# Low halves of plainly multiplied weight units: an adding transfer onto a negated copy instead of a subtraction on VectorE

## The chip, the cores and the metric

The kernel runs on one core of a Trainium2 chip. The metric is the device time of one execution in microseconds (us); lower is better. Engines are named as in the profile: PE (matmul) and PEld (its weight loads), DVE (VectorE), ACT (ScalarE), POOL (GpSimd), SP (SyncE, which issues most of the transfers here).

## The reference

One inference step of a decoder of two layers, for a prompt of 512 positions and a sample group of 8 x 8 positions, together 576 columns, with a model width of 1024. What matters here is where the large matrix products are:

```python
def sqrelu_mlp(x, w_up, w_down):
    return jnp.square(jax.nn.relu(x @ w_up)) @ w_down
...
    for l in range(DEPTH):
        i = l // 2
        if l % 2 == 0:
            y, s1, wk1, r1 = ab_mixer(x, ...)      # RWKV-7 heads and retention heads
        else:
            y, c1 = conv_mixer(x, ...)             # W_out(B * conv3(C * (W_in x)))
        x = layer_norm(ALPHA * x + y, ln1_g[l], ln1_b[l])
        x = layer_norm(ALPHA * x + sqrelu_mlp(x, w_up[l], w_down[l]), ln2_g[l], ln2_b[l])
```

The hidden width of the MLP is 4096. Inputs, weights and results are float32.

## The kernel before

**Precision.** PE multiplies operands of the type fp32r, a float32 that is rounded when it is written. To keep more of float32 every operand is held as a pair: `hi` is the value rounded to fp32r (a copy on ACT), `lo` is the value less `hi` (a subtraction on DVE). Both are made in `parts` (L72 to L79). A product of two pairs is three matmuls, in `mm3` (L150 to L154): hi by hi (L152), hi by the other's lo (L153), and the weight's lo by hi (L154). So a weight unit's `lo` is first read by the third matmul of its first step.

**Units.** The weights stand in HBM as units of 128 x 1024 numbers (512 KB), numbered in the order of use; a unit holds 8 blocks (k = 0 to 7) of 128 x 128 and makes 128 rows of a result. The columns are worked in two halves of 288 (g = 0, 1). A plain unit is 2 x 8 x 3 = 48 matmuls.

**Two phases.** Units 0 to 37 belong to the mixers of the first layer, a phase of its own that loads in half units; the change does not touch it. The second phase begins with unit 38 (`start_at(38)`, L1503): first MLP (38 to 101), convolution layer (102 to 133), second MLP (134 to 197). `mlp` (L1605) goes in four quarters, each with 8 units of the up-projection and 8 of the down-projection, and `res_evac` adds each result to the residual; the last unit of the last quarter is followed by a layer norm (`ln_add`, `ln_finish`).

**Plain and paired units.** Two units next to each other can be multiplied by a scheme with 7 products instead of 8 (`gemm7`, `steps7`), which needs sums of weight blocks. Such pairs are prepared in `prepare` (L117): POOL and DVE form sums at L123, then `parts` splits the results. All other units are multiplied as they are, in `gemm` (L156). Plain are the first four units of each MLP (38 to 41 and 134 to 137), all down-projections (46 to 53, 62 to 69, 78 to 85, 94 to 101, and the same in the second MLP), units 102 to 107 and 126 to 133 of the convolution layer. The up-projections of the quarters, and 108 to 125, are pairs.

**How a plain unit is prepared.** `gemm` calls `ensure` for units a little ahead; `ensure_` (L87) takes the next unit, gets a pair of buffers from `wtile` (or, for units 102 to 104 and 134 to 137, from `spots`, which are buffers of x that are free at that time), calls `load_to` (L48) so that SP loads up to three units ahead (L59) into three `raw` buffers, and calls `parts` on the raw copy. `parts` works in two chunks of four blocks (`chunk` is 4, from CH at L1285 and L1506): ACT copies 128 x 512 (L77), DVE subtracts 128 x 512 (L78), twice. In this phase there are five pairs of weight buffers `wh`, `wl` (WA + WB at L1291), which plain units use in turn with the pairs, and a pair of units takes three of them.

**The order of the work.** The tile framework orders each engine's instructions at build time with a simulated time line, by the order in which the code emits them and by when their operands are ready; on the chip each engine then works through its list in order, and semaphores hold it where an operand is late. So an instruction that waits holds up all that stand behind it on its engine. Preparation is emitted ahead of use and so tends to run as soon as a buffer comes free. `gate` (L83) keeps the preparations after a norm from running ahead of it.

**Where POOL works in this phase.** POOL makes the sums at L123 for the pairs, two of the seven combinations of each pair (L205), the subtractions of the mean at the norm (L255), its running sums (L273), products at L310, and sums of x at L1564. It issues few transfers: most are issued by SP.

Of the kernel before, what the change touches and what calls it, by code (L numbers as in the profile page):

```python
# [10 lines left out]
F32 = mybir.dt.float32  # L11
F32R = mybir.dt.float32r
AF = mybir.ActivationFunctionType
ALU = mybir.AluOpType
PSUM = bass.MemoryType.PSUM

P = 128
NT = 576
GN = 288
KT = 8  # L20
# [4 lines left out]
class Trunk:  # L25
# [61 lines left out]
    def ensure_(self, u, half=False):  # L87
        nc = self.nc
        u = min(u, self.nu - 1)
        while self.done <= u:  # L90
            if self.done in self.pairs:
                if self.half is None:
                    self.half = self.prepare(self.done)
                    next(self.half)
                if half: break
                for _ in self.half: pass
                self.half = None
                self.done += 2
                continue
            sp = []  # L100
            if self.halves:
                p = self.p_wsp[0]
                for h in range(2):
                    hi = p.tile([P, KT // 2, P], F32R, tag="wh", name="wh")
                    lo = p.tile([P, KT // 2, P], F32R, tag="wl", name="wl")
                    self.load_to(2 * self.done + h + 1)
                    self.parts(hi, lo, self.raw.pop((self.done, h)).rearrange("p (k m) -> p k m", m=P))
                    sp += [(hi[:, k], lo[:, k]) for k in range(KT // 2)]
            else:
                hi, lo = self.spots.get(self.done) or self.wtile()  # L110
                self.load_to(2 * self.done + 7)
                self.parts(hi, lo, self.raw.pop((self.done, 0)).rearrange("p (k m) -> p k m", m=P))
                sp = [(hi[:, k], lo[:, k]) for k in range(KT)]
            self.split[self.done] = sp
            self.done += 1
# [1595 lines left out]
```

## Time and profile before

| | |
|---|---|
| median of the runs shown | 1574.73 us (1573.41 to 1576.05, two runs) |
| the profiled execution | 1570.47 us |
| its span, first to last instruction | 1568.7 us |
| mean granted PE clock | 0.968 |
| second phase | from 484 us to the end |
| HBM read | 124.39 MB |

The profile records one execution. Three things help in reading it. An engine's share of busy time is an average over stages with different limits, so the windows by stage matter more. PE's matmuls overlap: a group's mean of some 297 ns is the time of one from start to end, while they start some 0.13 us apart at full clock. And what ended the idle time before an instruction is named behind it: `<-DMA raw<-in_w` means that a load into a raw buffer came last.

The tiles that the text names are `raw` (a loaded unit), `wh` and `wl` (hi and lo of a weight unit), `ht` and `lt` (hi and lo of a unit in one of the spots; the same names also stand for the sums of x), `hh`/`hl`, `he`/`le`, `ho`/`lo` (pairs of x or of hidden values), `acc` (a result in PSUM), `ln`, `u`, `x` (the norm).

### The profile page before, as it was taken

Reading aid. Unit: us, or ns where it says so; the run is one execution under the profiler, and the core shown is the slowest. Engines: PE = TensorE matmul, PEld = TensorE weight load, DVE = VectorE, ACT = ScalarE, POOL = GpSimd, SP = SyncE. Lnnn points to the kernel's source line nnn. Section 1 sums busy time; section 2 is a strip of 40 time slices with the busy share of each in tenths; the row PEclk is TensorE's granted clock in tenths of the full one; section 3 lists DMA queues with packets and bytes.
Section 4 is the critical chain, followed back from the end, with each engine's and each line's share of the span. In section 5 each row is a group of like instructions: output and inputs, shape, how many; then the busy total and the mean of one; then the engine's idle time right before and its main releaser. Section 6 shows DMA issues by size and latency. Waiting matters only on the chain.

```text
span 1568.7 us, 29898 instructions
## 1 busy us (share of the span) xinstructions
PE 1476.0 (94%) x11760; PEld 1421.9 (91%) x11760; DVE 1077.6 (69%) x2038; ACT 639.8 (41%) x1345; POOL 564.0 (36%) x643
## 2 busy tenths in 40 slices
PE   6999999998997889999999998989998999999995
PEld 6999898987886689999999997889988999999995
DVE  4656766675756795664846779899799575574755
ACT  4444334332233553342624545434365244251533
POOL 2032213336443551211302377555564121121355
PEclk9999999999898889999999999999999999999998
DMA  5333234435223013231322411223402314132221
GB/s 171 96 96 91 86 101 130 139 92 168 82 64 120 0 43 121 81 122 57 106 81 68 135 42 56 74 74 115 129 1 81 97 66 135 54 121 68 83 66 61
DMA packets 71197, 140.04 MB, mean 89 GB/s; under 512 B 21744, under 2 KB 31200, under 8 KB 71056
## 3 DMA queue, kind: packets, MB, share of 16 engines
q1 hardware_dynamic: 68224, 129.69, 26.6%
q0 software_dynamic: 1536, 5.57, 1.1%
q10 hardware_dynamic: 1296, 2.86, 0.6%
q8 instruction: 92, 1.51, 0.4%
q14 instruction: 49, 0.40, 0.1%
HBM read 124.39 MB, written 13.70 MB: 88 GB/s over the span
## 4 chain that ended last, share of the span: by engine, by line
PE 77%; DVE 11%; DMA 4%; POOL 4%; issue 3%; ACT 1%; SPq 1%; DVEq 0%; ACTq 0%; POOLq 0%
PE acc L152 21%; PE acc L153 21%; PE acc L154 21%; DVE wl L78 2%; PE mx L803 2%; DMA raw<-in_w 1%; DVE u L309 1%; POOL x L255 1%; DVE hl L78 1%; PE mx L700 1%; PE wa L152 1%; PE mx L542 1%; PE pq L283 1%; PE ps L283 1%; PE wa L154 1%
## 5 line engine op out<-in xcount | busy, mean ns | idle before, releaser
L77 ACT CAST wh<-raw 128x512 fp32r<-128x512 f32 x440 | 252.7, 618 | 411.2 <-PE acc L153 269.7
L78 DVE TENSOR_TENSOR wl<-raw,wh 128x512 fp32r<-128x512 f32 x440 | 330.2, 782 | 42.2 <-ACT wh L77 34.9
L153 PE MATMUL acc<-hl,wh 128*128 128x288 f32 x1180 | 349.0, 297 | 7.1 <-DVE hl L78 7.1
L154 PE MATMUL acc<-hh,wl 128*128 128x288 f32 x1180 | 348.6, 297 | 0.0
L152 PE MATMUL acc<-hh,wh 128*128 128x288 f32 x1180 | 344.4, 297 | 2.3 <-DVE ta L205 1.8
L153 PEld LDWEIGHTS acc<-hl,wh 128*128 128x128 f32 x1180 | 222.9, 189 | 8.0 <-DVE hl L78 7.5
L152 PEld LDWEIGHTS acc<-hh,wh 128*128 128x128 f32 x1180 | 221.2, 189 | 3.2 <-DVE ta L205 2.0
L154 PEld LDWEIGHTS acc<-hh,wl 128*128 128x128 f32 x1180 | 223.0, 189 | 0.3
L152 PE MATMUL acc<-xh,wh 128*128 128x288 f32 x480 | 148.3, 310 | 13.4 <-ACT xh L1395 12.4
L123 POOL TENSOR_TENSOR s<-raw 128x512 f32<-128x512 f32 x37 | 56.0, 1515 | 272.4 <-DMA raw<-in_w 206.1
L153 PE MATMUL acc<-xl,wh 128*128 128x288 f32 x480 | 146.2, 305 | 0.0
L154 PE MATMUL acc<-xh,wl 128*128 128x288 f32 x480 | 146.0, 304 | 0.0
L152 PE MATMUL acc<-ht,wh 128*128 128x288 f32 x444 | 130.9, 296 | 1.7 <-ACT wh L77 1.3
L153 PE MATMUL acc<-lt,wh 128*128 128x288 f32 x444 | 130.7, 295 | 0.0
L154 PE MATMUL acc<-ht,wl 128*128 128x288 f32 x444 | 130.5, 295 | 0.0
L123 POOL TENSOR_TENSOR raw<-raw 128x512 f32<-128x512 f32 x37 | 54.6, 1475 | 157.0 <-DVE raw L123 106.6
L152 PEld LDWEIGHTS acc<-xh,wh 128*128 128x128 f32 x480 | 91.5, 191 | 16.7 <-ACT xh L1395 12.8
L153 PE MATMUL acc<-lo,wh 128*128 128x288 f32 x352 | 105.2, 299 | 0.0
L152 PE MATMUL acc<-ho,wh 128*128 128x288 f32 x352 | 104.9, 300 | 0.1
L154 PE MATMUL acc<-ho,wl 128*128 128x288 f32 x352 | 104.9, 299 | 0.0
L153 PEld LDWEIGHTS acc<-xl,wh 128*128 128x128 f32 x480 | 91.5, 191 | 2.6 <-DVE xl L1396 0.7
L154 PEld LDWEIGHTS acc<-xh,wl 128*128 128x128 f32 x480 | 91.6, 191 | 1.5 <-issue 0.2
(461 smaller groups left out, 3498.0 us busy)
## 6 DMA issues: line engine op xcount, KB each, us to landing
raw<-in_w SPq DMA_DIRECT2D x160, 512.0 KB, 3.9
raw<-in_w SPq DMA_DIRECT2D x60, 256.0 KB, 2.9
A<-stg SPq DMA_DIRECT2D x9, 288.0 KB, 2.4
x<-in_x POOLq DMA_DIRECT2D x8, 288.0 KB, 7.4
out_y<-x SPq DMA_DIRECT2D x16, 144.0 KB, 1.8
wr<-in_w SPq DMA_DIRECT2D x16, 128.0 KB, 2.3
wr<-in_w SPq DMA_DIRECT2D x32, 64.0 KB, 2.0
kr<-A SPq DMA_DIRECT2D x6, 288.0 KB, 2.7
```

The costliest lines, as they stand in the source:

```text
L77: a = self.nc.scalar.copy(hi[:, s], src[:, s])
L78: b = self.nc.vector.tensor_tensor(out=lo[:, s], in0=src[:, s], in1=hi[:, s].bitcast(F32), op=ALU.subtract)
L123: tt = lambda e, o, x, y, op: e.tensor_tensor(out=o, in0=x, in1=y, op=op)
L152: nc.tensor.matmul(acc, lhsT=hi, rhs=xh, start=first, stop=False)
L153: nc.tensor.matmul(acc, lhsT=hi, rhs=xl, start=False, stop=False)
L154: nc.tensor.matmul(acc, lhsT=lo, rhs=xh, start=False, stop=last)
L255: e.tensor_tensor(out=t, in0=t, in1=c, op=ALU.subtract)
L283: self.nc.tensor.matmul(st[k], lhsT=self.ones1024, rhs=t, start=start, stop=stop)
L309: nc.vector.tensor_tensor(out=u, in0=r, in1=mn, op=ALU.subtract)
L542: self.nc.tensor.matmul(ps, lhsT=lhsT, rhs=rhs[:, o:o + n], start=True, stop=True)
L700: nc.tensor.matmul(both[h][:, i], lhsT=b3[q, c, h:h + 2].rearrange('p s t -> p (s t)'), rhs=la[q, c], start=True, stop=True)
L803: nc.tensor.matmul(ps[:, i], lhsT=bd(self.mb if n < 3 else self.Y0, j + i), rhs=v[:, j + i], start=True, stop=True)
```

## The change

For plain units of the second phase `lo` is made in another way. ACT copies the raw unit to `hi` as before, then writes the negative of `hi` into `lo` (a second ACT operation for each chunk). Then one transfer, issued by POOL, reads the same unit from HBM once more and adds it onto `lo` in place (`accum_op=ALU.add`), so that `lo` ends as the weight less `hi`. DVE has no part in it. The raw buffer is now released by ACT's copy and no longer by DVE's subtraction. The load into `raw` stays. Pairs, the splits of x and of hidden values, and the first phase go on with `parts`.

```diff
             else:
                 hi, lo = self.spots.get(self.done) or self.wtile()
                 self.load_to(2 * self.done + 7)
-                self.parts(hi, lo, self.raw.pop((self.done, 0)).rearrange("p (k m) -> p k m", m=P))
+                src = self.raw.pop((self.done, 0)).rearrange("p (k m) -> p k m", m=P)
+                for i in range(0, KT, 4):
+                    a = nc.scalar.copy(hi[:, i:i + 4], src[:, i:i + 4])
+                    nc.scalar.activation(lo[:, i:i + 4], hi[:, i:i + 4].bitcast(F32), AF.Copy, scale=-1.0)
+                b = nc.gpsimd.dma_start(lo.rearrange('p k m -> p (k m)'), self.w_all[self.done].bitcast(F32R), accum_op=ALU.add)
+                self.last = [a.ins, b.ins]
                 sp = [(hi[:, k], lo[:, k]) for k in range(KT)]
             self.split[self.done] = sp
             self.done += 1
```

## The prediction

> **What bounds the kernel now.** First the busy times of the whole span, then the same by stages, because an average hides where an engine waits. A row by stage gives the window, its length, then the busy time of PE, PEld, DVE, ACT and POOL, the granted clock, the DMA share and GB/s.
>
> ```profile
> PE 1476.0 (94%) x11760; PEld 1421.9 (91%) x11760; DVE 1077.6 (69%) x2038; ACT 639.8 (41%) x1345; POOL 564.0 (36%) x643
> ```
> ```profile
> 484.00:500.00 16.00, 11.41 (x59) 8.85 (x58) 11.98 (x24) 6.80 (x15) 3.37 (x8) 0.79 0.75 235
> ...
> 604.00:892.00 288.00, 288.00 (x2175) 287.79 (x2174) 177.73 (x303) 114.03 (x208) 57.46 (x50) 1.00 0.29 90
> ...
> 940.00:964.00 24.00, 16.70 (x100) 15.77 (x99) 23.93 (x31) 12.33 (x27) 19.33 (x18) 0.86 0.20 67
> ...
> 1204.00:1516.00 312.00, 312.00 (x2356) 311.79 (x2355) 197.94 (x336) 129.90 (x236) 65.14 (x58) 1.00 0.29 94
> ...
> sum 1085.00, PE 1024.85 PEld 1007.41 DVE 772.61 ACT 465.80 POOL 404.74; mean PE 68.32 PEld 67.16 DVE 51.51 ACT 31.05 POOL 26.98
> ```
>
> The change touches only the second phase, from 484 us on. In two long stages (288 and 312 us) PE never stops at full clock, while DVE works 62% and 63% of the time. Relief for DVE is worth nothing there. In all the phase PE is idle 1085 - 1025 = 60 us, around the layer norms and in the convolution; that is the ceiling of any gain, and 940 to 964 is a place where DVE is full (23.93 of 24) and PE is not.
>
> The weights are the second thing to read: who waits for them, and how long before PE needs them they are made.
>
> ```profile
> SPq L59 <- DVE wl L78: 889.6, 140, 75.0
> ```
> ```profile
> ACT wh L77 <- PE acc L153: 269.7, 108, 5.7
> ```
>
> The loads wait for DVE to release a raw slot; the casts wait for PE to release a pair of weight buffers. So a weight unit's preparation starts when PE frees a buffer, and the time from then to its first use is fixed by the five buffers, not by DVE.
>
> **What is removed.** In the issues below, 160 units are loaded in this phase, and the pair sums on POOL (L123) number 37, so 74 units go in pairs and 86 plainly. Each plain unit has two subtractions at L78.
>
> ```profile
> raw<-in_w SPq DMA_DIRECT2D x160, 512.0 KB, 3.9
> raw<-in_w SPq DMA_DIRECT2D x60, 256.0 KB, 2.9
> ```
> ```profile
> L77 ACT CAST wh<-raw 128x512 fp32r<-128x512 f32 x440 | 252.7, 618 | 411.2 <-PE acc L153 269.7
> L78 DVE TENSOR_TENSOR wl<-raw,wh 128x512 fp32r<-128x512 f32 x440 | 330.2, 782 | 42.2 <-ACT wh L77 34.9
> L123 POOL TENSOR_TENSOR s<-raw 128x512 f32<-128x512 f32 x37 | 56.0, 1515 | 272.4 <-DMA raw<-in_w 206.1
> ```
>
> 172 subtractions x 0.782 us = 134.5 us leave DVE, most of it in the stages where PE is full: worth nothing there. The two places where plain subtractions lie on the chain that sets the end are these (rows of the chain and of DVE):
>
> ```profile
> 949.49 3.12 ACT wh L77 x6
> ...
> 954.22 0.35 ACT ho L77
> 954.59 3.74 DVE wl L78 x3
> ...
> 961.18 1.53 DVE lo L78
> ```
> ```profile
> 1088.61 2.43 DVE wl L78 x2
> ...
> 1095.01 0.72 DVE wl L78
> ```
>
> At 949 units 105 to 107 are prepared ahead of the last splits of x, for which PE waits. Without the subtractions DVE is free for the splits, but ACT has six negations more (six x 0.57 = 3.4 us) ahead of the casts that these splits need; the last of those ends at 954.6, so now near 958.0, and the split that started at 961.18 starts there: **-3.2 us**. Bounds: 0 (POOL, with three issues between its sums, is late instead) and -7.4 (all six subtractions). At 1088 to 1095.7 the chain loses up to 2.43 + 0.72 = 3.2 us, but unit 126's own landing is due there; see below.
>
> **What is added.** On ACT, 172 negations 128x512. No such row exists; a cast of that size is 618 ns, two in a row take 1.14 us in the rows below, so 0.57 each, 98 us in all. ACT stands at 41% of the span, and in the long stages at 114 of 288 us: hidden by its idle time. On POOL, 86 issues at about 0.54 us (first row), 46 us in all; in the long stages POOL is busy 57 of 288 us: hidden too. On the DMA engines, 86 x 512 KB again; their share there is 0.29, so even at double price (source and destination read) there is room: hidden.
>
> ```profile
> L1427 POOL DMA_DIRECT2D x<-in_x x8 | 4.3, 541 | 5.1 <-PE acc L154 5.1
> ```
> ```profile
> s<-in_wkv POOLq DMA_DIRECT2D x4, 256.0 KB, 4.0
> ...
> lw<-in_lw POOLq DMA_DIRECT2D x1, 768.0 KB, 10.5
> ```
>
> **The disputed price: when does lo land?** No adding transfer is in the trace. From SP 256 KB land in 2.9 us and 512 KB in 3.9 us; from POOL 256 KB land in 4.0 us, so 1.1 us later than from SP. A plain 512 KB from POOL would then take 5.0 us. The adding one also reads its destination: 512 KB more through the same engines, at SP's step of 1.0 us per 256 KB, is 2.0 us. Bounds: 5.0 us (the second read hides) and 10.5 us (the slowest POOL row). I take 6.5 us, three quarters of the second read, because raw loads share the engines.
>
> The Trainium skill, page "DMA: Bandwidth & Descriptors", section "Anatomy of one DMA — SWDGE (gpsimd) path", fits a transfer issued by GpSimd as 2.0 us plus bytes over 436,000 per us, an estimate of 3.2 us for this size. The trace does not bear that out: 256 KB already take 4.0 us here. By that price nothing below would be late, and the sum would be near -4 us (-3.2, another -3.2 at 1088, +2.0 at the start).
>
> From the start of a unit's casts to lo ready I count four ACT operations of 0.57 us, POOL's issue of 0.54, and 6.5 us: 2.9 + 6.5 = **9.4 us**. Before it was cast, then subtraction, some 2.5 us. Now the lead, at each passage from pairs to plain units (start of the first unit's casts; PE's first use; lo is read two matmuls later, 0.27 us):
>
> ```profile
> 676.53 1.14 ACT L77 CAST wh<-raw 128x512 fp32r<-128x512 f32 x2 [0.44 <-PE acc L153]
> ...
> 585.18 1.12 ACT L77 CAST wh<-raw 128x512 fp32r<-128x512 f32 x2
> ...
> 1203.45 3.23 ACT L77 CAST wh<-raw 128x512 fp32r<-128x512 f32 x6
> ...
> 1087.64 1.14 ACT L77 CAST wh<-raw 128x512 fp32r<-128x512 f32 x2 [1.47 <-DMA raw<-in_w]
> ...
> 903.30 1.14 ACT L77 CAST wh<-raw 128x512 fp32r<-128x512 f32 x2
> ```
> ```profile
> 687.53 0.30 PE L152 MATMUL acc<-hh,wh 128*128 128x288 f32 x1
> ...
> 592.25 0.30 PE L152 MATMUL acc<-hh,wh 128*128 128x288 f32 x1
> ...
> 1212.23 0.30 PE L152 MATMUL acc<-hh,wh 128*128 128x288 f32 x1
> ...
> 1096.15 0.40 PE L152 MATMUL acc<-hh,wh 128*128 128x288 f32 x1 [1.81 <-DVE ta L205]
> ```
> ```profile
> 911.11 0.46 DVE L257 TENSOR_TENSOR x<-x,acc 128x288 f32<-128x288 f32 x1 [2.39 <-PE acc L154]
> ```
>
> Unit 62 (and its five likes, in the other quarters of the two MLPs) has 11.0 + 0.27 = 11.3 us: hidden, by 1.9 us. Unit 46 has 592.52 - 585.18 = 7.3: late by **+2.1**. Unit 142, the third of the casts that start at 1203.45 (so at 1205.6), has 6.9: late by **+2.5**. Unit 126 has 8.8: **+0.6**, and the chain's 3.2 us on DVE are lost with it. Unit 101, the last before the first MLP's closing norm, is cast at 903.30; PE gets to it when the product before it is done and taken by DVE, at 911.11, so it has 8.1 us: +1.3, and 0.5 for the operation that POOL may be in: **+1.8**.
>
> PE also pays for the stall itself. After a long wait the chain shows 0.24 us per matmul instead of 0.13 for some 20 matmuls:
>
> ```profile
> 560.32 2.42 DVE hl L78 x2
> ...
> 563.40 0.24 PE acc L154
> ...
> 568.20 0.24 PE acc L153
> ...
> 568.62 0.13 PE acc L152
> ```
>
> From 563.40 to 568.62 some 21 matmuls lose 0.11 us each, 2.4 us. I charge this once, at unit 142, the longest of the stalls: **+2.4**. Bounds: 0 and twice that.
>
> **The start of the phase**, 484 to 500, has the DMA engines at 0.75 already, and units 38 to 41 bring 2 MB more, though PE needs none of it until the norm is done. POOL is the risk: it works in order, and what waits behind an issue is the norm:
>
> ```profile
> 499.32 1.52 POOL L123 TENSOR_TENSOR s<-raw 128x512 f32<-128x512 f32 x1 [5.84 <-DMA raw<-in_w]
> 500.81 5.34 POOL L255 TENSOR_TENSOR x<-x,ln 128x288 f32<-128x288 f32 x7
> ```
>
> Here the pair sum already stood 5.84 us at the head of POOL's queue and held up the norm's subtractions. Bounds: -1.5 (raw slots come free after the cast, so that the sum comes sooner) and +5 (an issue waits for the fourth unit's negation, which waits for its load). I take **+2.0**.
>
> **The sum:** -3.2 + 2.1 + 2.5 + 0.6 + 1.8 + 2.4 + 2.0 = **+8.2 us**. The profiled execution took 1570.5 us (span 1568.7); it becomes 1578.7. The median of the runs shown is 4.2 us above the profiled one, so I predict **1582.9 us**, 0.5% more. A difference under 2% (31 us) is about what a measurement of this kernel can't tell from none.
>
> **Rivals.** *Late landings everywhere (slower).* If lo takes 11.0 us from issue to landing instead of 6.5, unit 62's kind is late by 2.9 + 11.0 - 11.3 = 2.6 us, and each of six such passages costs 2.6 + 2.4 = 5.0, together 30 us; the four short ones get 4.5 us worse each, 18 us, and two more slow starts add 4.8. With the sum of +8.2 that is +61: 1636 us. The six begin to pay from 8.4 us on, and 2% are passed near 9.5. For it: 10.5 us at 768 KB, and the loads that run at the same passages. Against it: 4.0 us at 256 KB. *In time everywhere (a gain).* If lo lands within 4 us of its issue, every lateness vanishes, and what is left is -3.2 at 949, up to -3.2 at 1088 and nothing at the start: -6, so 1569 us. For it: the DMA engines are idle for 0.7 of the long stages. Against it: the same 4.0 us for half the bytes. The fit of the Trainium skill's page named above would give this case. *POOL held up at the norms.* If each of the four norms finds an issue that waits for ACT at the head of POOL's queue, as the pair sum at 499.32 did, and loses those 5.84 us each time, it adds 23.4 us less the 2.0 counted: 1604 us. Against it: the issue waits for ACT alone, which is idle half of the time at a norm (12.33 of 24 us busy from 940), while the pair sum waited for a load.
>
> **Chances.** The forecast 0.55 (1570 to 1598); in time everywhere 0.18; late landings 0.18; POOL held up 0.09. No case gains 31 us, and half of the 60 us of idle time would be needed: faster 0.02. Late landings end above 1606 nearly always, POOL held up in a third of cases: slower 0.20. Same 0.78. The range runs from 1564 (the gain with its larger bound) to 1618, which leaves out the worse half of the late landings.
>
> **What would show it.** Right: L78's weight rows fall by 172, PE stays full from 604 to 892, DMA landings from POOL near 6.5 us, PE waits for a DMA into wl at 592 and 1212 only, each of 2 to 4 us. Wrong: PE waiting for wl at 687 and its likes; landings of 10 us; POOL's queue standing at the head of a norm; or issues on POOL far above 0.54 us.

## The result, and the profile after

The changed kernel takes 1614.4 us (median of two runs, 1613.64 to 1615.16) against 1574.73 before: 2.6% more, ratio 1.0261, 95% interval 1.0233 to 1.029. That is 39.7 us, against a forecast of 8.2. The profiled execution has a span of 1613.4 us (before 1568.7), 44.7 more. The edit adds five lines above the rest, so in the changed kernel the three matmuls of a product are L157 to L159, the norm's subtractions L260 and the sums of x L1569; the new cast, negation and transfer are L114, L115 and L116.

First the engines over the whole span and the rows of the lines that the change touches.

```profile
PE 1490.2 (92%) x11760; PEld 1434.1 (89%) x11760; DVE 953.4 (59%) x1866; ACT 726.7 (45%) x1517; POOL 617.9 (38%) x729
...
L78 DVE TENSOR_TENSOR wl<-raw,wh 128x512 fp32r<-128x512 f32 x282 | 211.2, 781 | 39.9 <-ACT wh L77 33.5
...
L116 POOL DMA_DIRECT2D wl<-in_w x79 | 71.1, 912 | 184.8 <-ACT wl L115 160.7
```

DVE is relieved as planned: 124 us less, 158 subtractions fewer in this row, and 14 more in the units of the spots. It bought nothing. POOL's issue takes 0.912 us where 0.54 was assumed. Then the transfers: size and median time from issue to landing, and the time that the software queue's packets took as a share of 16 engines.

```profile
raw<-in_w SPq DMA_DIRECT2D x160, 512.0 KB, 4.6
...
wl<-in_w POOLq DMA_DIRECT2D x79, 512.0 KB, 8.4
```
```profile
q0 software_dynamic: 13920, 50.67, 16.3%
```

Low parts land after 8.4 us, not 6.5, and SP's own loads became slower, 4.6 us instead of 3.9. Now by stages (window, length, busy PE, PEld, DVE, ACT, POOL, granted clock, DMA share, GB/s) and PE's waits for these transfers (us in total, times, longest).

```profile
606.00:620.00 14.00, 12.62 (x84) 12.62 (x85) 2.14 (x4) 3.32 (x6) 1.72 (x2) 0.88 1.01 239
622.00:904.00 282.00, 282.00 (x2133) 282.00 (x2133) 147.53 (x250) 135.01 (x250) 75.39 (x72) 1.00 0.52 135
...
1250.00:1264.00 14.00, 11.13 (x72) 10.90 (x73) 1.88 (x3) 7.17 (x14) 3.22 (x4) 0.88 1.05 283
1264.00:1558.00 294.00, 294.00 (x2220) 293.79 (x2219) 149.15 (x258) 142.93 (x265) 80.94 (x79) 1.00 0.52 133
```
```profile
PE acc L159 <- DMA wl<-in_w: 18.2, 6, 4.2
```

The two long stages are as full as before, at full clock. The loss sits in short stretches: behind the first passage of each MLP the DMA engines have no room left (share 1.01 and 1.05), and PE stalls, and its mean granted clock in these two windows is 0.88. Six waits, 18.2 us together, stand where there were none. The timeline of PE names all six: at 607.38 (unit 46), 936.07 (unit 101), 990.77 (105), 1123.49 (126), 1163.80 (133) and 1252.82 (142).

Around the closing norm of the first MLP the chain that sets the end (start, us, what) ran through POOL's norm operations before as well:

```profile
890.23 9.58 POOL x L255 x10
...
900.64 4.00 POOL x L255 x4
```

Now transfers stand behind them on it:

```profile
907.54 2.68 POOL x L260 x4
...
911.12 1.61 POOL x L260 x3
...
914.22 4.75 POOL x L260 x7
...
919.53 0.80 POOL wl L116
...
924.85 11.08 DMA wl<-in_w
...
974.85 6.83 POOL ts L1569 x8
...
985.27 5.46 DMA wl<-in_w
```

Fourteen norm operations come first on POOL. Unit 100 is issued behind them at 919.53, and three units for the spots go out before unit 101 at 924.85. It lands 11.08 us later, in a burst of five. Sixty us later the same happens behind the sums of x at L1569: unit 105 is issued behind them and PE waits for it.

### The profile page after: what moved, and what is told of

The parts are those of the page before. It is cut to its first block, busy times and chain, and to the rows that moved or that the text cites. A ratio compares the mean times of both kernels' runs of the same rounds, so it can differ in the third digit from the quotient of the medians.

```text
span 1613.4 us, 30164 instructions
## 1 busy us (share of the span) xinstructions
PE 1490.2 (92%) x11760; PEld 1434.1 (89%) x11760; DVE 953.4 (59%) x1866; ACT 726.7 (45%) x1517; POOL 617.9 (38%) x729
## 3 DMA queue, kind: packets, MB, share of 16 engines
q0 software_dynamic: 13920, 50.67, 16.3%
q10 hardware_dynamic: 1296, 2.86, 0.6%
## 4 chain that ended last, share of the span: by engine, by line
PE 69%; DVE 10%; DMA 7%; POOL 6%; issue 5%; ACT 2%; SPq 1%; DVEq 0%; ACTq 0%; POOLq 0%
PE acc L159 19%; PE acc L157 19%; PE acc L158 19%; DMA wl<-in_w 3%; PE mx L808 2%; DVE wl L78 2%; DMA raw<-in_w 2%; DVE u L314 1%; PE wa L157 1%; POOL ts L1569 1%; POOL ln L278 1%; PE mx L705 1%; PE wa L159 1%; POOL s L128 1%; DVE u L315 1%
## 5 line engine op out<-in xcount | busy, mean ns | idle before, releaser
L159 PE MATMUL acc<-hh,wl 128*128 128x288 f32 x1180 | 351.2, 300 | 15.5 <-DMA wl<-in_w 15.4
L157 PE MATMUL acc<-hh,wh 128*128 128x288 f32 x1180 | 344.3, 298 | 1.2 <-ACT hh L77 0.6
L159 PEld LDWEIGHTS acc<-hh,wl 128*128 128x128 f32 x1180 | 225.2, 191 | 17.3 <-DMA wl<-in_w 10.5
L78 DVE TENSOR_TENSOR wl<-raw,wh 128x512 fp32r<-128x512 f32 x282 | 211.2, 781 | 39.9 <-ACT wh L77 33.5
L157 PEld LDWEIGHTS acc<-hh,wh 128*128 128x128 f32 x1180 | 223.0, 191 | 2.2 <-ACT hh L77 0.9
L157 PE MATMUL acc<-xh,wh 128*128 128x288 f32 x480 | 148.2, 310 | 13.7 <-ACT xh L1400 11.6
L159 PE MATMUL acc<-xh,wl 128*128 128x288 f32 x480 | 146.1, 304 | 0.0
L116 POOL DMA_DIRECT2D wl<-in_w x79 | 71.1, 912 | 184.8 <-ACT wl L115 160.7
L157 PE MATMUL acc<-ht,wh 128*128 128x288 f32 x444 | 130.9, 296 | 2.7 <-ACT wh L77 1.7
L159 PE MATMUL acc<-ht,wl 128*128 128x288 f32 x444 | 130.5, 294 | 0.0
L114 ACT CAST wh<-raw 128x512 fp32r<-128x512 f32 x158 | 89.9, 617 | 84.0 <-PE acc L158 79.9
L157 PEld LDWEIGHTS acc<-xh,wh 128*128 128x128 f32 x480 | 91.4, 191 | 17.1 <-ACT xh L1400 12.0
L157 PE MATMUL acc<-ho,wh 128*128 128x288 f32 x352 | 105.4, 301 | 0.1
L159 PE MATMUL acc<-ho,wl 128*128 128x288 f32 x352 | 104.8, 298 | 0.0
```

The lines of the kernel that those rows point to most:

```text
L78: b = self.nc.vector.tensor_tensor(out=lo[:, s], in0=src[:, s], in1=hi[:, s].bitcast(F32), op=ALU.subtract)
L114: a = nc.scalar.copy(hi[:, i:i + 4], src[:, i:i + 4])
L116: b = nc.gpsimd.dma_start(lo.rearrange('p k m -> p (k m)'), self.w_all[self.done].bitcast(F32R), accum_op=ALU.add)
L157: nc.tensor.matmul(acc, lhsT=hi, rhs=xh, start=first, stop=False)
L159: nc.tensor.matmul(acc, lhsT=lo, rhs=xh, start=False, stop=last)
```

## The experiments

My theory after the result: the loss is lateness at the places with a short lead, made by a landing that is dearer than assumed and by POOL's order. Rivals: a price for every unit (traffic, ACT, POOL), the negations on ACT, or the adding itself. All edits below are to the changed kernel unless said otherwise. Each time is the median of 4 to 10 runs, with the kernel before on the same chip beside it (1573.8 to 1574.6 us).

**Where it is lost.** Five kernels use the new way for one group of the plain units each, and the old `parts` for the rest. Together the groups hold all 86. (In these kernels the lines stand a little lower again: the transfer is L117 and the third matmul L162.)

```diff
-                src = self.raw.pop((self.done, 0)).rearrange("p (k m) -> p k m", m=P)
...
+                if any(q <= self.done < q + 8 for q in (62, 78, 158, 174)):
...
+                else:
+                    self.parts(hi, lo, self.raw.pop((self.done, 0)).rearrange("p (k m) -> p k m", m=P))
```

The other four have this condition instead: `self.done < 42`; `46 <= self.done < 54 or 142 <= self.done < 150`; `94 <= self.done < 105 or 126 <= self.done < 138 or 190 <= self.done`; `105 <= self.done < 108`.

The long leads, 32 units:

> The new way only in the 32 plain units with the long lead (the second, third and fourth quarter of each MLP, units 62, 78, 158, 174 and the seven behind each), the old way in the other 54. My theory: they are hidden behind 11 us of lead, so 1572 to 1579 us, like the kernel before. Rival, a price per unit wherever it stands (traffic, ACT, POOL): 32 of 86 units would give 15 us, 1587 to 1592.

Measured 1573.8 us against 1574.26, ratio 0.9999 (0.9986 to 1.0012). The transfers land no sooner than in the whole change, and PE is still full:

```profile
wl<-in_w POOLq DMA_DIRECT2D x32, 512.0 KB, 8.2
```
```profile
604.00:890.00 286.00, 286.00 (x2164) 286.00 (x2163) 157.64 (x268) 128.28 (x236) 68.72 (x64) 1.00 0.44 119
```

A price for each unit is out: 32 units at 8.2 us cost nothing where the lead hides them.

The phase start:

> The new way only in units 38 to 41, the four that are prepared at the phase start (484 to 512). My theory: POOL's issues and the traffic of 2 MB more hold up the norm's tail; by the milestones of the two traces 5 to 9 us, so 1580 to 1584 us. Rival, these units cost nothing by themselves (PE needs them only after the norm) and the delay there comes from the first phase: 1573 to 1577 us.

Measured 1576.45 us against 1574.55, ratio 1.0016 (1.0 to 1.0032): 1.9 us, at most 5. My number was too high. I had read it from the two traces by absolute times, and a good part of that difference arises in the first phase, whose code is the same (last section).

The first quarters:

> The new way only in units 46 to 53 and 142 to 149, the first quarter of each MLP. My theory: unit 46 and unit 142 land late, each a stall and a half-clock step, 5.9 and 5.4 us by the milestones: 1584 to 1588 us. Rival, the lateness there is inherited from the order of work behind a late norm: 1573 to 1579 us.

Measured 1585.61 us, ratio 1.0069 (1.0048 to 1.0091): +11.1 us, as expected. PE's waits show the two late units:

```profile
PE acc L162 <- DMA wl<-in_w: 6.9, 2, 4.1
```

The landing time alone does not tell the price: its median is 9.7 us in this kernel, and 10.9 us for the four units of the phase start, which cost 1.9 us together.

The tails of the norms:

> The new way only in units 94 to 104, 126 to 137 and 190 to 197, the plain units around the second, third and last norm. My theory: POOL's fourteen norm operations stand ahead of the issues, and the last units land 9 to 11 us after them; by the milestones 10.6, 9.5 and 3.7 us, with 1 to 3 for unit 126: 1596 to 1603 us, the largest share of the loss. Rival, the delays there need the other units' traffic as well: under 1588 us.

Measured 1601.88 us, ratio 1.0175 (1.0153 to 1.0196): +27.3 us, the largest share by far, with no help from the other units' traffic.

Units 105 to 107:

> The new way only in units 105 to 107 at the end of the attention stage. My theory: the splits of x end 3 us sooner, as predicted, but unit 105 lands late and PE stalls for 3 us with a half-clock step behind it, and later waits on DVE take back what is left: 1573 to 1578 us. Rival, relief of DVE is worth its 3 us or more: 1569 to 1572 us. Rival, the transfers cost more than they free: 1579 us or more.

Measured 1574.13 us, ratio 0.9997 (0.9981 to 1.0012): nothing. The timelines show why. Of before (the norm's logarithm on ACT as a common mark, and the last splits of x on DVE):

```profile
939.35 0.45 ACT L297 ACTIVATE w<-ln 128x288 f32<-128x288 f32 x1 [2.20 <-DVE ln L294]
```
```profile
961.18 1.52 DVE L78 TENSOR_TENSOR lo<-x,ho 128x288 fp32r<-128x288 f32 x1
963.05 0.45 DVE L78 TENSOR_TENSOR lo<-x,ho 128x288 fp32r<-128x288 f32 x1
```

Of this kernel:

```profile
941.14 0.45 ACT L305 ACTIVATE w<-ln 128x288 f32<-128x288 f32 x1 [2.20 <-DVE ln L302]
```
```profile
958.98 1.06 DVE L78 TENSOR_TENSOR lo<-x,ho 128x288 fp32r<-128x288 f32 x1
963.03 0.45 DVE L78 TENSOR_TENSOR lo<-x,ho 128x288 fp32r<-128x288 f32 x1
```
```profile
967.47 0.61 PE L162 MATMUL acc<-he,wl 128*128 128x288 f32 x1 [2.88 <-DMA wl<-in_w]
```

From the norm's logarithm to these two splits it took 21.8 and 23.7 us before, and 17.8 and 21.9 now: DVE is 1.8 to 4.0 us sooner, as predicted. PE then waits 2.88 us for unit 105's transfer. The gain in this trace was real and was spent at once.

The five differences, -0.5 + 1.9 + 11.1 + 27.3 - 0.4, make 39.4 us; the whole change costs 39.7. By their intervals each of the five is known to some 2 to 3.4 us, so the sum, an estimate, could be off by about 6. Within that the places add up, and no price that all units share is needed.

**What it is made of.** The same transfer without the adding:

```diff
-                b = nc.gpsimd.dma_start(lo.rearrange('p k m -> p (k m)'), self.w_all[self.done].bitcast(F32R), accum_op=ALU.add)
+                b = nc.gpsimd.dma_start(lo.rearrange('p k m -> p (k m)'), self.w_all[self.done].bitcast(F32R))
```

> The transfer onto the negated part is kept with its issue, its bytes and its waits, but it overwrites instead of adding, so the low part is the weight itself (the subtraction is left out of the computation). My theory: the changed kernel loses its 40 us because low parts land late where the lead is short; part of that landing time (5.4 us alone, median 8.4) is the adding's second read of the same bytes. Without it I expect a median landing of 6 to 7 us and 1590 to 1602 us, 12 to 25 us less than the changed kernel. Rival A, the order of POOL's queue and the issue's length (0.86 to 0.9 us) make it late, not the adding: landings near 8 us stay and the time is 1608 to 1616. Rival B, nearly all is the adding: landings of 4 to 5 us and 1575 to 1585.

Measured 1587.6 us, ratio 1.0092 (1.0057 to 1.0127, so 9 to 20 us above the kernel before): 26.8 of the 40 us are gone. It lies between my range and rival B's. Issue, landing and engine time, and then unit 46's issue on POOL and PE's wait for it:

```profile
L116 POOL DMA_DIRECT2D wl<-in_w x79 | 43.3, 549 | 188.5 <-ACT wl L115 159.3
...
wl<-in_w POOLq DMA_DIRECT2D x79, 512.0 KB, 5.1
```
```profile
q0 software_dynamic: 13920, 50.67, 10.0%
```
```profile
589.21 0.59 POOL L116 DMA_DIRECT2D wl<-in_w  x1 [6.62 <-ACT wl L115]
```
```profile
594.22 0.40 PE L159 MATMUL acc<-hh,wl 128*128 128x288 f32 x1 [1.15 <-DMA wl<-in_w]
```

The changed kernel at the same place:

```profile
599.36 0.89 POOL L116 DMA_DIRECT2D wl<-in_w  x1 [6.64 <-ACT wl L115]
```
```profile
607.38 0.61 PE L159 MATMUL acc<-hh,wl 128*128 128x288 f32 x1 [4.17 <-DMA wl<-in_w]
```

It is nearly a clean pair: POOL was released alike (6.6 us of waiting for the negation), and from issue to PE's first use it is 5.0 us without the adding and 8.0 with it. PE's wait grows from 1.15 to 4.17, by the same 3.0 us. For the same bytes the adding costs 3.3 us of landing (median 5.1 to 8.4), 0.36 us of issue, and more engine time: 16.3% of 1613.4 us against 10.0% of 1582.0. The kernel with the norms on DVE (below) has no such transfers and spends 1.1% of its 1572.5 us on the queue's other work:

```profile
q0 software_dynamic: 1536, 5.57, 1.1%
```

So a unit takes (263.0 - 17.3) / 86 = 2.86 us of all 16 engines with the adding and (158.2 - 17.3) / 86 = 1.64 without: 1.74 times as much. The Trainium skill, page "Collectives: The Full Stack", section "The bandwidth ceiling: the fold count and why AG ≠ RS ≠ AR", says of a collective, the ReduceScatter between cores, that it is slower than the copying AllGather for the add's two source reads and not for the arithmetic, and gives a measured ratio of 1.93. The 1.74 here goes the same way; that the second read is the cause was not tried by itself.

The negations alone, with DVE adding the raw weight and no transfer:

```diff
-                b = nc.gpsimd.dma_start(lo.rearrange('p k m -> p (k m)'), self.w_all[self.done].bitcast(F32R), accum_op=ALU.add)
+                    b = nc.vector.tensor_tensor(out=lo[:, i:i + 4], in0=src[:, i:i + 4], in1=lo[:, i:i + 4].bitcast(F32), op=ALU.add)
```

> The negations on ACT stay, the transfer goes, and DVE adds the raw weight onto the negated part (172 operations of the size of the old subtractions). My theory: the negations hide in ACT's idle time nearly everywhere, so this runs like the kernel before, 1574 to 1582 us; the 1 to 5 us above it are the added step at the places where preparation is on the chain (949, 585). Rival, ACT pays a good part of the loss because its negations stand ahead of the casts at the norms: 1590 or more.

Measured 1580.39 us, ratio 1.0045 (1.0031 to 1.006): 6.1 us by the medians, near the upper end of my range. It is a price of its own, and small. Where it is paid was not found: in this trace no matmul of PE waits for a low part made in this way. To see whether it is ACT's load, the negations of the changed kernel went to DVE:

```diff
-                    nc.scalar.activation(lo[:, i:i + 4], hi[:, i:i + 4].bitcast(F32), AF.Copy, scale=-1.0)
+                    nc.vector.tensor_scalar(out=lo[:, i:i + 4], in0=hi[:, i:i + 4].bitcast(F32), scalar1=-1.0, scalar2=None, op0=ALU.mult)
```

> The changed kernel with the negations on DVE, where the old subtractions stood, instead of on ACT; transfers as they are. If the 6 us that the negations cost without transfers are ACT's (they stand ahead of casts), they come back: 1606 to 1611 us. If they came from the order on DVE, or if the transfers hide them, nothing changes: 1612 to 1618 us.

Measured 1617.91 us, ratio 1.0275 (1.0241 to 1.0309): nothing comes back. The rival that ACT's load is the cause has no support here, though these transfers may hide a gain of a few us.

**Landing time or POOL's order, at the tails?** The tails kernel without the adding, by the same edit:

> The new way in the same tail units, but the transfer overwrites instead of adding (the subtraction is left out, so those low parts are the weights themselves). Theory B (the adding's longer landing and issue): the price falls as in the whole kernel, to a third, 7 to 12 us, 1582 to 1587 us. Theory A (POOL's order decides): 3.3 us less landing at each of three tails gives back 10 us, and the price is 15 to 20, 1590 to 1595 us.

Measured 1584.73 us, ratio 1.0074 (1.0047 to 1.0102): the price of the tails falls from 27.3 to 10.9 us, as theory B had it. Then POOL's order. First a control, the kernel before with the norm's subtractions on DVE:

```diff
-                e = G if x in cf['pg'] else V
+                e = V
```

> A control: the kernel before, with the norms' fourteen subtractions of the mean on DVE instead of POOL (at three of the four norms). DVE gets 14 x 0.46 = 6.4 us per norm, POOL loses 11.3. Expected 1570 to 1582 us; it is wanted as the base of the next kernel, and if it came out below 1570 it would be a gain of its own.

Measured 1573.68 us against 1573.82, ratio 1.0004 (0.999 to 1.0019): no gain and no loss. The same line in the tails kernel:

> The new way in the tail units (94 to 104, 126 to 137, 190 to 197) and the norms' subtractions on DVE, so that the issues of units 100, 101, 196 and 197 no longer stand behind them on POOL. Against its control. Theory A (POOL's order is a good part of the tails' price): the price falls from 27.3 us to 12 to 19, since the third norm has no such operations and keeps its 9. Theory B (the landing time alone): the price stays at 23 to 28.

Measured 1592.92 us, 19.2 above its control, where it was 27.3. Theory A asked for 12 to 19, B for 23 to 28: the result stands just above A's range. So a part of the price, some 8 us, is POOL's order (each of the two times is known to about 3.5 us), and it stands beside the landing time. What is left shows in POOL's timeline (unit 101's issue, behind three for the spots from 905.98 on) and in PE's:

```profile
913.17 1.74 POOL L117 DMA_DIRECT2D wl<-in_w  x1
```
```profile
924.22 0.58 PE L162 MATMUL acc<-hh,wl 128*128 128x288 f32 x1 [4.49 <-DMA wl<-in_w]
```

Counted from the norm's first sum in each trace, unit 101 is issued 3.2 us sooner than in the tails kernel (15.8 us behind it against 19.0) and read 3.9 us sooner (26.9 against 30.8). But it is still read only 11 us after its issue, in the burst with the spots' units, and PE, which now gets there sooner, waits 4.49 us for it (1.97 in the tails kernel). A version that keeps the spots' units out of this burst was not tried.

**Can it start sooner?** Two transfers for each unit, each behind its own half's negation:

```diff
-                b = nc.gpsimd.dma_start(lo.rearrange('p k m -> p (k m)'), self.w_all[self.done].bitcast(F32R), accum_op=ALU.add)
+                    b = nc.gpsimd.dma_start(lo[:, i:i + 4].rearrange('p k m -> p (k m)'), self.w_all[self.done][:, i * P:(i + 4) * P].bitcast(F32R), accum_op=ALU.add)
```

> Two transfers of 256 KB for each unit, each behind its own half's negation, instead of one of 512 KB. My theory (lateness at short leads): the first half starts 1.2 us sooner and lands some 2 to 3 us sooner, and PE reads it first, so the stalls shrink: 1595 to 1606 us. Rival (POOL's queue): 86 issues more, each 0.6 to 0.9 us, stand on POOL where norms and pair sums wait for it, and the time stays or grows: 1612 to 1630 us.

Measured 1613.32 us, ratio 1.0251 (1.0224 to 1.0279): the rival's value, and mine is refuted.

```profile
L116 POOL DMA_DIRECT2D wl<-in_w x158 | 143.8, 1116 | 124.7 <-ACT wl L115 113.6
...
wl<-in_w POOLq DMA_DIRECT2D x158, 256.0 KB, 8.2
```
```profile
PE acc L159 <- DMA wl<-in_w: 10.8, 11, 3.3
```

PE's waits for the transfers fall from 18.2 to 10.8 us, but half the bytes land no sooner (8.2 us), an issue takes 1.116 us, and POOL's issues take 144 us instead of 71. What PE gains there, 7.4 us, it loses elsewhere: three of its waits around norms grow by 6.3 us together (2.91 to 6.67 for a cast of x behind the first MLP's norm, 2.84 to 3.91 and 2.94 to 4.43 for the sums of the last norm). That POOL's added issues cause this is inferred and not tried.

No experiment points to a version that beats the kernel before: the best parts of the change, the long leads and units 105 to 107, are worth nothing.

## Why the prediction was right and wrong, point by point

The forecast, 1582.9 us, is 31.5 us too low. That the range to 1618 holds the result is owed to its width and not to the mechanism: the upper part was there for the rival of late landings everywhere, which did not come; the forecast's own 1570 to 1598 misses, and "slower" had 0.20 against 0.78 for "same". The remark that 2% can hardly be told from none was wrong too, since the result is known to 1.0233 to 1.029. The prediction has the sign and the steady stages. Three terms failed: the landing, the list of places, and the time from cast to issue. Of its own signs of being right, POOL's landings near 6.5 us and waits at two places only did not come; of its signs of being wrong, issues far above 0.54 us and some landings over 10 us did.

**The landing price: the step that failed first.** "I take 6.5 us, three quarters of the second read." The plain part was right: 5.0 us for 512 KB from POOL was worked out, 5.1 measured. The surcharge for the adding was put at 1.5 us; it is 3.3 at the median, with single landings of up to 12.9 us, and 0.36 us of issue on top. The experiment without the adding puts 26.8 of the 39.7 us on it. The Trainium skill's fit on the page "DMA: Bandwidth & Descriptors", section "Anatomy of one DMA — SWDGE (gpsimd) path", by which 3.2 us is the estimate for this size, is not borne out here even without the adding, 5.1 us beside other loads.

**The list of places: the second.** The sum had 2.4 us for units 101 and 126 (1.8 and 0.6) and nothing for unit 133, where PE then waits 3.59 us, or for the last norm, where PE waits for no transfer but for its two sums it waits 3.3 us longer (2.84 and 2.94 us against 1.31 and 1.20 before). The tails cost 27.3. For unit 101 the text counted 8.1 us of lead and "0.5 for the operation that POOL may be in". In fact its cast starts at 915.85, its negation is done at 920.26, and its issue follows at 924.85:

```profile
915.85 1.13 ACT L114 CAST wh<-raw 128x512 fp32r<-128x512 f32 x2
...
919.12 1.14 ACT L115 ACTIVATE wl<-wh 128x512 fp32r<-128x512 f32 x2
```

POOL is held by the fourteen norm operations until 919.5, and then works off unit 100, three spots' transfers and some of the norm's sums before unit 101. From cast to issue it is 9.0 us instead of 2.3, of which 4.6 on POOL, and 11.2 from issue to use instead of 7.0. The same text had quoted this line's operations at the first norm (L255, x7), and had a rival in which a norm waits behind an issue. It never asked the reverse: what an issue waits behind.

**The first quarters.** Predicted 2.1 + 2.5 + 2.4 = 7.0, measured 11.1. The lead at unit 46 was right: its cast starts at 594.38, and its first matmul at 601.45, so by the prediction's count lo was wanted 7.3 us after the cast. It was read after 13.0 us (607.38) where 9.4 was counted. From issue to use it took 8.0 us instead of 7.0. The rest is the step from cast to issue: 2.3 us was counted for four ACT operations, and it took 5.0 (594.38 to 599.36). PE then stood idle 4.17 us and not 5.7, since its list has other matmuls of this unit ahead of the first with lo. Between cast and issue ACT's list has two splits of the hidden values, casts of the next unit and a copy:

```profile
594.38 1.13 ACT L114 CAST wh<-raw 128x512 fp32r<-128x512 f32 x2
595.41 0.67 ACT L77 CAST hh<-ta 128x576 fp32r<-128x576 f32 x1
595.99 0.67 ACT L77 CAST hh<-tb 128x576 fp32r<-128x576 f32 x1
596.57 0.63 ACT L115 ACTIVATE wl<-wh 128x512 fp32r<-128x512 f32 x1
597.10 1.13 ACT L114 CAST wh<-raw 128x512 fp32r<-128x512 f32 x2
598.13 0.39 ACT L218 COPY s<-acc 128x288 f32<-128x288 f32 x1
598.42 1.16 ACT L115 ACTIVATE wl<-wh 128x512 fp32r<-128x512 f32 x2
```
```profile
601.45 0.30 PE L157 MATMUL acc<-hh,wh 128*128 128x288 f32 x1
```

**The steady passages.** Predicted hidden, and so they were (-0.5 us), though it took a landing of over 8 us. At unit 62 the cast starts at 690.08, the issue at 692.61, and PE's first use is at 702.66:

```profile
690.08 1.14 ACT L114 CAST wh<-raw 128x512 fp32r<-128x512 f32 x2 [0.93 <-PE acc L158]
```
```profile
692.61 0.86 POOL L116 DMA_DIRECT2D wl<-in_w  x1
```
```profile
702.66 0.30 PE L157 MATMUL acc<-hh,wh 128*128 128x288 f32 x1
```

That leaves 10.3 us from the issue to the first use of lo. The prediction's own count left 8.4 (11.3 less 2.9), just the median landing that was measured; that the trace has two us more here was not foreseen. It is why the rival of late landings, which wanted 30 us more from six such passages, was right on the landing at the bad places and wrong on these.

**At 949,** -3.2 was predicted. In the kernel with units 105 to 107 alone the splits do come 1.8 to 4.0 us sooner, but not quite as counted: the cast for the first of them runs ahead of the six negations (955.91, they start at 956.24), only the one for the second behind them (959.88). PE then waits for unit 105's transfer, for which the sum had no term: -0.4.

**The phase start,** +2.0 predicted, +1.9 measured (0 to 5): right in size, but the way that was named does not show: no issue holds up the norm. In the trace of the changed kernel POOL's pair sum still waits for its load (5.54 us, 5.84 before), the norm's subtractions behind it, and the pair sum starts 7.0 us behind the norm's first sum (501.73) where it was 1.9 before (497.47):

```profile
508.72 1.26 POOL L128 TENSOR_TENSOR s<-raw 128x512 f32<-128x512 f32 x1 [5.54 <-DMA raw<-in_w]
```

**The half clock** was charged once, 2.4 us. There are six stalls on the transfers, each over 2 us. Behind the one at 607.38 matmuls are 0.24 us apart until 610.67, some 13 of them at 0.11 us more, 1.4 us. Behind four others it is 12 to 24 matmuls; behind the one at 936.07 the step is 0.13 at once. Together they are some 85 matmuls, 9 us, an estimate; no run tells this part from the stalls. With the 18.2 us of waits it makes some 27 of the 44.7 us by which this trace is longer; 4.3 arise in the first phase, up to the first norm's first sum (501.73 against 497.47), and the rest was followed only in part.

**Relief for DVE is worth nothing** in the long stages: right, 124 us left DVE and PE is full as before.

## What to carry to other kernels

Before work is moved to a transfer, write down for every place of use the lead, and what stands ahead of the issue on the issuing engine, not only what waits behind it. Here the short leads at stage ends decided, and a landing of over 8 us cost nothing where the lead was long. A transfer that adds is not a plain one with a small surcharge: here it landed 3.3 us later at the median and took 1.74 times the engine time. And an engine that is not the bottleneck, relieved by 124 us, gave nothing back, while each of six late operands cost a stall and five of them a slow restart.

## What was not expected of the hardware

**Half the bytes, the same landing.** Adding transfers of 256 KB landed after 8.2 us at the median, those of 512 KB after 8.4, and the issue of a half took 1.116 us, more than that of the whole, 0.912. Which part of this is the fuller queue was not tried.

**The length shown for an issue is not the time that POOL is held.** Unit 46's issue in the changed kernel, at 599.36, is shown with 0.89 us, and the next POOL operation starts 0.61 us behind its start:

```profile
599.97 1.11 POOL L210 TENSOR_TENSOR ta<-ta,s 128x288 f32<-128x288 f32 x1
```

**Equal code, unequal time.** The first norm's first sum, behind the phase that no kernel here changes, starts at 494.74 us in the kernel without the adding and at 505.33 in the one with the negations alone:

```profile
494.74 1.33 PE L251 MATMUL cps<-x,o 128*128 128x288 f32 x2 [0.67 <-DVE x L1343]
```
```profile
505.33 1.33 PE L251 MATMUL cps<-x,o 128*128 128x288 f32 x2 [1.35 <-DVE x L1343]
```

Ten us between single executions is more than most terms of the sum. So the price of a place is read from its own start in each trace, or from the medians of many runs.
